# A depthwise convolution computed on even and odd tokens apart, in three half-length filters, without POOL and later in the program

## The chip, the cores and the metric

The program runs on one core of a Trainium2 chip. A core has a matmul engine (PE, with its weight loads shown apart as PEld), three engines for elementwise work (DVE, ACT and POOL) and a queue, SP, that starts most of the transfers from HBM. Each engine works through its own list of instructions in the order in which they stand there, and waits on semaphores for the others. The metric is the time of one execution on the device, in microseconds; lower is better.

## What is computed

One layer of a decoder: 1024 tokens of 1024 channels. A combined input projection feeds four token mixers (a convolution module, latent attention, causal pooling, a gated MLP over chunks); each mixer's output is normalized and goes through its part of `w_out`; a dense squared-ReLU MLP and a last norm follow. The part that the change touches is the convolution module, on 256 of the projected channels (`a`) and 256 gates (`g`):

```python
def conv_module(z, dw_w, dw_b, ln_g, ln_b, pw_w):
    a, g = jnp.split(z, 2, axis=-1)
    y = a * jax.nn.sigmoid(g)
    y = lax.conv_general_dilated(                  # 31 taps, causal, per channel
        y, dw_w[:, None, :], window_strides=(1,), padding=[(CONV_KERNEL - 1, 0)],
        dimension_numbers=('NWC', 'WIO', 'NWC'), feature_group_count=GROUP_WIDTH) + dw_b
    y = jax.nn.silu(layer_norm(y, ln_g, ln_b))
    return y @ pw_w
```

## The kernel before

Everything is float32; a matrix product is made of three matmuls on operands that were split into a high and a low part (`split`: ACT writes the high part, DVE the low one), so each weight that is loaded costs one ACT and one DVE instruction before PE can use it.

The program has two parts. The dense MLP is written in an order made out by hand, from the first product `ffe` on. All that comes before it (projections, mixers, `w_out`) is ordered by a scheduler: the code states what is to be done and in which order of priority, `tc.high_priority(offset=n)` moves a stretch of it ahead by n, and the scheduler lays the instructions of each engine out in one fixed list. Tiles come from rings with few buffers (the tag `K` has 4, `raw` for weights as they come from HBM has 2, `e` and `N` have 1), and a tile takes its turn in its ring.

The names that matter here, in the order in which the work runs:

- `zc`: the products of the convolution's input projection, in four pieces (two groups of 128 channels, `i`, by two halves of the tokens, `hf`). `conv_gate` (L245 to L250) makes the gated input `ycv0`, `ycv1` of them, 128 channels by 1024 tokens each.
- the taps. `tap0` (L313) writes `acc0`, `acc1` = first tap plus bias on ACT, one half of the tokens at a time. A further tap is one DVE instruction, `acc = ycv * weight + acc` on 512 tokens (`conv_taps`, L332, its instruction L337), or, for some taps of group 1, an ACT product into `tap` and an add on POOL (`pool_taps`, L324): 7 taps of the first half and 13 of the second (`NPT`). Of the 120 further taps that leaves 100 for DVE and 20 for POOL. `conv_taps` of the first half stands early in the program with an offset of 2000, that of the second further on with 4000.
- `zp`: the pooling mixer's projection; `zgm` and `zml`: the input projections of the gated MLP and of attention, four products of 48 matmuls each. Their weights `zgm0` to `zgm3`, `zml0` to `zml3` are split as they come. `evac_mla` scales what `zml` gives, `gate` and `ogT` belong to the gated MLP.
- `conv_ln(u)` (L538) for u = 0 to 3, 256 tokens each: PE transposes `acc` (`lnb`), DVE takes mean and variance (`bst`, `bmv`), POOL the root (`lnr`), DVE normalizes (`yn`), PE transposes back (`lnT`), ACT and DVE finish the silu (`vh`, `th`) and split the result into `us`.
- `conv_out` multiplies `us` with the pointwise weights `cw` (`pwc` on PE); `wo` are the products with `w_out`, added to `h` on DVE (L475), `py`, `pw`, `oTp` the pooling mixer's, `cT`, `tl`, `kb`, `qb` attention's preparations.

Of the kernel before, what the change touches and what calls it, by code (L numbers as in the profile page):

```python
# [7 lines left out]
F32 = mybir.dt.float32  # L8
# [9 lines left out]
NRAW = 2  # L18
NB = 8
NM = 2  # L20
NPT = (7, 13)
NWARM = 16
T = 1024
NT = T // P
# [4 lines left out]
GW = 256  # L29
CK = 31  # L30
# [15 lines left out]
C_DWB = 6  # L46
# [11 lines left out]
C_DWW = 61  # L58
# [19 lines left out]
def _trunk(tc, nc, act, dve, pool, pe, sb, ps, hbm, a):  # L78
# [4 lines left out]
    def const(shape, name, dt=F32):  # L83
        return sb.tile(shape, dt, tag=name, name=name)
# [3 lines left out]
    def U(tag, name, shape, dt=F32):  # L88
        return sb.tile([P] + shape, dt, tag=tag, name=name, bufs=BUFS[tag])
# [83 lines left out]
    cols = const([P, NCOL], "cols")  # L173
    ident = const([P, P], "ident")
# [5 lines left out]
    lnhalf = const([P, 4], "lnhalf")  # L180
# [60 lines left out]
    ycv = [None, None]  # L241
    acc = [None, None]

    def conv_gate(i, hf, ba, bg):
        sl = slice(hf * 512, (hf + 1) * 512)  # L245
        th = M("th", [512])
        dve.tensor_mul(th, bg, rb[:, sl])
        dve.scalar_tensor_tensor(ycv[i][:, sl], ba, 0.5, rb[:, sl], ALU.mult, ALU.mult)
        act.activation(th, th, AF.Tanh, scale=0.5)
        dve.scalar_tensor_tensor(ycv[i][:, sl], th, 1.0, ycv[i][:, sl], ALU.add, ALU.mult)  # L250

    wraw, wcm = [], []
    for i in range(2):
# [33 lines left out]
    rb = U("P", "rb", [T])  # L287
# [10 lines left out]
    dve.tensor_scalar(lnhalf, cols[:, C_LNG:C_LNG + 4], 0.5, None, ALU.mult)  # L298

    for i in range(2):  # L300
        ycv[i] = U("P", "ycv%d" % i, [T])
    conv_gate(0, 0, b[:, 0:512], b[:, 512:])
    for i, hf in ((1, 0), (0, 1), (1, 1)):
        if (i, hf) == (0, 1):
            ba, bg = K("zc"), O("zc")
        else:
            b = X("zc")
            ba, bg = b[:, 0:512], b[:, 512:]
# [4 lines left out]
    def tap0(i, hf):  # L313
        if hf == 0:
            acc[i] = U("K", "acc%d" % i, [T])
        sl = slice(hf * 512, (hf + 1) * 512)
        act.activation(acc[i][:, sl], ycv[i][:, sl], AF.Identity,  # L317
                       scale=cols[:, C_DWW + i * CK + CK - 1:C_DWW + i * CK + CK], bias=cols[:, C_DWB + i:C_DWB + i + 1])

    def lag(i, k, hf):  # L320
        lo, hi = max(k, hf * 512), (hf + 1) * 512
        return cols[:, C_DWW + i * CK + CK - 1 - k:C_DWW + i * CK + CK - k], ycv[i][:, lo - k:hi - k], acc[i][:, lo:hi]

    def pool_taps(hf, n):  # L324
        for k in range(1, n + 1):
            c, ya, aa = lag(1, k, hf)
            tap = U("Z", "tap", [512])[:, :ya.shape[1]]
            act.activation(tap, ya, AF.Copy, scale=c)  # L328
            pool.tensor_tensor(aa, aa, tap, ALU.add)  # L329

    def conv_taps(hf, n):
        todo = [(0, k) for k in range(1, CK)]  # L332
        for j, k in enumerate(range(n + 1, CK)):
            todo.insert(2 * j + n + 1, (1, k))
        for i, k in todo:
            c, ya, aa = lag(i, k, hf)
            dve.scalar_tensor_tensor(aa, ya, c, aa, ALU.mult, ALU.add)  # L337

    for hf in range(2):
        tap0(0, hf)  # L340
        tap0(1, hf)
        pool_taps(hf, NPT[hf])

    zp = [None, None]
    for i in range(2):
        w = load_w(a["w_cm"][4 + i], 1024, "wp%d" % i)
        b = X("zp")
# [8 lines left out]
        pool.tensor_scalar(dst[rows, :sh], src[rows, :sh], 1.0, 0.0, ALU.mult, ALU.add)  # L356

    def window_out(win, i):
        rc = small(16, "rc16", 2)
        dve.tensor_mul(rc, win[:, 0:16], cols[:, C_RC + 16 * i:C_RC + 16 * (i + 1)])  # L360
        dve.tensor_sub(rc, rc, zp[i][:, 0:16])
        dve.scalar_tensor_tensor(zp[i], win, cols[:, C_INVW + i:C_INVW + i + 1], zp[i], ALU.mult, ALU.subtract)
        dve.tensor_copy(zp[i][:, 0:16], rc)
# [169 lines left out]

    us = [None, None]

    def conv_ln(u):
        hf = u // 2
        b = K("lnb")  # L538
        for j in range(2):
            for ct in range(2):  # L540
                pe.transpose(b[:, j * GW + ct * P:j * GW + (ct + 1) * P],
                             acc[ct][:, (2 * u + j) * P:(2 * u + j + 1) * P], ident)
        st = small(12, "bst", 2)
        mv = small(4, "bmv", 2)
        for j in range(2):
            dve.bn_stats(st[:, 6 * j:6 * j + 6], b[:, j * GW:(j + 1) * GW])
            dve.bn_aggr(mv[:, 2 * j:2 * j + 2], st[:, 6 * j:6 * j + 6])
        rs = rstd(mv.rearrange("p (j c) -> p j c", c=2)[:, :, 1], 2, "lnr")
        yn = M("yn", [2 * GW])
        for j in range(2):  # L550
            dve.tensor_scalar(yn[:, j * GW:(j + 1) * GW], b[:, j * GW:(j + 1) * GW], mv[:, 2 * j:2 * j + 1],
                              rs[:, j:j + 1], ALU.subtract, ALU.mult)
        b = O("lnT")
        for ct in range(2):
            for j in range(2):
                pe.transpose(b[:, ct * GW + j * P:ct * GW + (j + 1) * P], yn[:, j * GW + ct * P:j * GW + (ct + 1) * P],
                             ident)
        vh = M("vh", [2, GW])
        for ct in range(2):
            act.activation(vh[:, ct, :], b[:, ct * GW:(ct + 1) * GW], AF.Identity, scale=lnhalf[:, ct:ct + 1],  # L560
                           bias=lnhalf[:, 2 + ct:3 + ct])
        th = M("th2", [2, GW])
        act.activation(th, vh, AF.Tanh)
        dve.scalar_tensor_tensor(vh, th, 1.0, vh, ALU.add, ALU.mult)
# [284 lines left out]

    def spare(name):  # L850
        return sb.tile([P, 2, 512], F32, tag="CS", name=name, bufs=1)[:, 0]

    def E(name):
        return sb.tile([P, 512], F32, tag="e", name=name, bufs=1)

    def dram(name, n, dt=F32):
        return hbm.tile([P, n], dt, tag=name, name=name, bufs=1)
# [413 lines left out]
        z_load("zml", 0)  # L1271
    load_h(1)
    with tc.high_priority(offset=2000):
        conv_taps(0, NPT[0])
        z_load("zml", 2)
    with tc.high_priority(offset=1000):
        load_h(2)
# [345 lines left out]
```

## Time and profile before

| | |
|---|---|
| time, median of 3 runs | 1052.73 us (1049.21 to 1052.87) |
| the profiled execution's own time | 1050.52 us |
| its span, from the first to the last instruction | 1048.7 us |
| instructions | 13388 |
| busy: PE, DVE, ACT, POOL | 95%, 81%, 48%, 24% of the span |

The page cuts the span into 40 slices of 26 us; the scheduled part fills the first 15. A group of instructions is given with its count, its busy time, the mean of one, and the idle time of its engine just ahead of it with what ended that. PE's busy time is long by construction: a matmul counts until its result has landed, so neighbours overlap; how fast PE really advances is read from the distance of starts.

### The profile page before, as it was taken

How to read it: one execution, taken by the hardware profiler on the slowest of the kernel's cores; microseconds unless marked ns; L12 is line 12 of the kernel's file. 1: busy time of each engine (PE TensorE's matmuls, PEld its weight loads, DVE VectorE, ACT ScalarE, POOL GpSimd, SP SyncE). 2: the span in 40 equal slices, each digit the busy share in tenths (PEclk: the TensorE clock that was granted, in tenths of full speed). 3: DMA queues.
4: the chain of work that ended last, by engine and by line, in shares of the span. 5: the costliest groups of instructions: out<-in, count | busy, mean ns of one | idle time of the engine just before them, and what ended most of it. 6: DMA issues, size and time to landing. Idle time of an engine off the chain costs nothing.

```text
span 1048.7 us, 13388 instructions
## 1 busy us (share of the span) xinstructions
PE 996.6 (95%) x4674; PEld 819.9 (78%) x4674; DVE 845.9 (81%) x1275; ACT 503.4 (48%) x937; POOL 247.0 (24%) x334
## 2 busy tenths in 40 slices
PE   9994899999999999978999999998999999999996
PEld 7883689888888887756888887886888888888885
DVE  4999999998888666775777775665898988988987
ACT  7641147546568766554445554553251341341334
POOL 0459558323232312211212211221000000000004
PEclk9997899999999999998999999999999999999999
DMA  9411024211002006864666665549949249248004
GB/s 334 155 60 39 30 58 181 78 41 41 1 1 82 1 1 225 302 225 170 232 241 233 228 221 200 202 170 390 392 152 330 81 154 328 81 164 337 1 1 161
DMA packets 49492, 165.71 MB, mean 158 GB/s; under 512 B 6032, under 2 KB 7952, under 8 KB 49424
## 3 DMA queue, kind: packets, MB, share of 16 engines
q1 hardware_dynamic: 36288, 119.68, 32.7%
q0 software_dynamic: 12992, 45.10, 11.1%
q8 instruction: 37, 0.61, 0.2%
q14 instruction: 31, 0.25, 0.1%
q10 hardware_dynamic: 144, 0.07, 0.1%
HBM read 113.45 MB, written 51.38 MB: 157 GB/s over the span
## 4 chain that ended last, share of the span: by engine, by line
PE 65%; DVE 15%; issue 8%; DMA 6%; POOL 3%; ACT 3%; SPq 0%; POOLq 0%; DVEq 0%; ACTq 0%
PE ffb L160 17%; PE ffx L160 13%; PE ffa L160 12%; PE ffy L160 8%; DVE acc L337 8%; PE wo L160 4%; PE ob L160 2%; PE s L676 2%; DMA raw_b<-in_w_ff 1%; PE ptb L719 1%; PE woa L160 1%; DMA xin<-in_x 1%; PE qb L160 1%; DMA wp_raw<-in_w_cm 1%; DVE h L475 1%
## 5 line engine op out<-in xcount | busy, mean ns | idle before, releaser
L160 PE MATMUL ffb<-wop,fop 128*128 128x512 f32 (+1 forms) x780 | 181.4, 392 | 1.0 <-DVE h L1083 1.0
L160 PEld LDWEIGHTS ffb<-wop,fop 128*128 128x128 f32 x780 | 145.2, 188 | 35.5 <-DVE h L1083 1.2
L160 PE MATMUL ffx<-hnT,wop 128*128 128x512 f32 x624 | 151.6, 396 | 5.8 <-ACT ffx L1014 5.0
L160 PEld LDWEIGHTS ffx<-hnT,wop 128*128 128x128 f32 x624 | 118.5, 190 | 33.1 <-ACT ffx L1014 5.5
L160 PE MATMUL ffa<-wop,fop 128*128 128x512 f32 x576 | 137.1, 397 | 3.8 <-DVE h L1083 3.8
L884 DVE TENSOR_TENSOR wop<-w_raw,wop 128x512 fp32r<-128x512 f32 x112 | 76.1, 688 | 72.3 <-ACT wop L881 72.3
L160 PEld LDWEIGHTS ffa<-wop,fop 128*128 128x128 f32 x576 | 109.3, 190 | 29.6 <-DVE h L1083 4.2
L881 ACT ACTIVATE wop<-raw_b 128x512 fp32r<-128x512 f32 x96 | 59.5, 623 | 123.6 <-PE ffa L160 38.4
L337 DVE SCALAR_TENSOR_TENSOR acc<-ycv,cols,acc 128x512 f32<-128x512 f32 (+22 forms) x100 | 99.6, 1038 | 0.6 <-ACT acc L317 0.3
L881 ACT ACTIVATE wop<-w_raw 128x512 fp32r<-128x512 f32 x112 | 68.8, 626 | 43.9 <-DVE w_raw L1027 20.7
L160 PE MATMUL ffe<-hnT,wop 128*128 128x512 f32 x288 | 71.1, 402 | 8.8 <-ACT m L980 8.8
L881 ACT ACTIVATE fop<-raw_f 128x512 fp32r<-128x512 f32 x64 | 39.8, 622 | 75.1 <-DVE h_back L1083 27.6
L884 DVE TENSOR_TENSOR wop<-raw_b,wop 128x512 fp32r<-128x512 f32 x96 | 65.7, 684 | 10.4 <-ACT wop L881 9.7
L1238 POOL TENSOR_SCALAR mr_ms<-mssq,epsr 128x1 f32<-128x1 f32 x7 | 2.8, 399 | 296.9 <-ACT fjunk L1236 296.9
L160 PEld LDWEIGHTS ffe<-hnT,wop 128*128 128x128 f32 x288 | 54.2, 192 | 22.4 <-ACT m L980 10.9
L160 PE MATMUL ffy<-hnB,wop 128*128 128x512 f32 x192 | 46.8, 392 | 0.0
L160 PE MATMUL ffy<-hnT,wop 128*128 128x512 f32 x192 | 46.5, 391 | 0.0
L958 POOL DMA_DIRECT2D fs<-fst x48 | 25.8, 538 | 84.4 <-DVE fst L131 81.0
L884 DVE TENSOR_TENSOR fop<-raw_f,fop 128x512 fp32r<-128x512 f32 x64 | 44.0, 687 | 0.0
L160 PEld LDWEIGHTS ffy<-hnB,wop 128*128 128x128 f32 x192 | 36.0, 188 | 8.2
L160 PEld LDWEIGHTS ffy<-hnT,wop 128*128 128x128 f32 x192 | 36.1, 188 | 7.9
L329 POOL TENSOR_TENSOR acc<-acc,tap 128x512 f32<-128x512 f32 (+7 forms) x20 | 35.2, 1760 | 29.0 <-ACT tap L328 27.7
(450 smaller groups left out, 2153.2 us busy)
## 6 DMA issues: line engine op xcount, KB each, us to landing
fs<-fst POOLq DMA_DIRECT2D x48, 512.0 KB, 3.4
fop<-fs SPq DMA_DIRECT2D x48, 512.0 KB, 6.9
w_raw<-in_w_ff SPq DMA_DIRECT2D x44, 512.0 KB, 4.1
raw_b<-in_w_ff SPq DMA_DIRECT2D x32, 512.0 KB, 5.8
raw_f<-fr SPq DMA_DIRECT2D x32, 512.0 KB, 5.5
fr<-s POOLq DMA_DIRECT2D x32, 256.0 KB, 3.2
fr<-f POOLq DMA_DIRECT2D x20, 256.0 KB, 2.4
xin<-in_x SPq DMA_DIRECT2D x8, 512.0 KB, 8.4
```

The source lines that it names most:

```text
L160: pe.matmul(out, lhs(x), rhs(y), start=start and i == 0, stop=stop and i == 2, skip_group_check=more)
L329: pool.tensor_tensor(aa, aa, tap, ALU.add)
L337: dve.scalar_tensor_tensor(aa, ya, c, aa, ALU.mult, ALU.add)
L475: dve.scalar_tensor_tensor(h[t], b, rs, h[t], ALU.mult, ALU.add)
L676: pe.matmul(sb_[:, c0:c0 + w], q[:, x, qo:qo + P], kt[:, y, 0:w], start=i == 0, stop=i == 2 and not last)
L719: pe.transpose(b[:, place[j] + s * P:place[j] + (s + 1) * P], pts[s][:, (2 * kp + j) * P:(2 * kp + j + 1) * P], ident)
L881: act.activation(self.t[:, 0], self.src(), AF.Copy)
L884: dve.tensor_sub(self.t[:, 1], self.src(), high(self.t))
L958: pool.dma_start(fs[p][q], t.rearrange("p x c -> p (x c)").bitcast(F32))
L1238: pool.tensor_scalar(ms, ssq, 1.0 / D, epsr[:, t:t + 1], ALU.mult, ALU.add)
```

## The change

The 1024 tokens of `ycv` are kept as two rows of 512, even tokens `x0` and odd ones `x1`. With the filter split likewise into even and odd taps, the even outputs are the even taps on `x0` plus the odd taps on `x1` one place back. The odd outputs are not made of two more half-length filters but of one: the even and odd taps are added beforehand (`hsum`, 15 pairs of weights for each group, L331), that filter runs on `x0 + x1`, and the two other results are subtracted. So a group of channels takes three chains of 14 or 15 taps on 512 tokens, in place of four of 15 or 16. The first tap of a chain, where it is a product only, is made on ACT (`acc`, `conv_b`).

No tap goes to POOL any more. `conv_gate` writes `ycv` token pair by token pair, `conv_ln` reads every transposed block from one of the rows, and its `vh` puts even and odd tokens together again. `conv_b` takes the buffer `e`, which had been used by the MLP part alone.

The taps lose both offsets: the whole convolution, with `conv_ln(0)` to `conv_ln(2)` behind it, now stands after the load of `wkv`, far down in the program.

```diff
-NPT = (7, 13)
...
-        dve.scalar_tensor_tensor(ycv[i][:, sl], ba, 0.5, rb[:, sl], ALU.mult, ALU.mult)
+        dve.scalar_tensor_tensor(ba, ba, 0.5, rb[:, sl], ALU.mult, ALU.mult)
         act.activation(th, th, AF.Tanh, scale=0.5)
-        dve.scalar_tensor_tensor(ycv[i][:, sl], th, 1.0, ycv[i][:, sl], ALU.add, ALU.mult)
+        dve.scalar_tensor_tensor(ycv[i].rearrange("p c n -> p n c")[:, hf * 256:(hf + 1) * 256],
+                                 th.rearrange("p (n c) -> p n c", c=2), 1.0,
+                                 ba.rearrange("p (n c) -> p n c", c=2), ALU.add, ALU.mult)
...
-    for hf in range(2):
-        tap0(0, hf)
-        tap0(1, hf)
-        pool_taps(hf, NPT[hf])
...
+    def chain(out, src, taps):
+        for k, c in taps:
+            dve.scalar_tensor_tensor(out[:, k:], src[:, 0:512 - k], c, out[:, k:], ALU.mult, ALU.add)
+
+    def conv_even_odd(i):
+        acc[i] = U("K", "acc%d" % i, [2, 512])
+        x0, x1 = ycv[i][:, 0], ycv[i][:, 1]
+        y0, y1 = acc[i][:, 0], acc[i][:, 1]
+        b = E("conv_b")
+        act.activation(y0, x0, AF.Copy, scale=tap(i, 0))
+        act.activation(b, x1, AF.Copy, scale=tap(i, 1))
+        chain(y0, x0, [(k, tap(i, 2 * k)) for k in range(1, CK // 2 + 1)])
+        chain(b, x1, [(k, tap(i, 2 * k + 1)) for k in range(1, CK // 2)])
+        bias = cols[:, C_DWB + i:C_DWB + i + 1]
+        dve.scalar_tensor_tensor(y1, y0, bias, b, ALU.subtract, ALU.add)
+        dve.tensor_scalar(y0[:, 0:1], y0[:, 0:1], bias, None, ALU.add)
+        dve.scalar_tensor_tensor(y0[:, 1:], y0[:, 1:], bias, b[:, 0:511], ALU.add, ALU.add)
+        dve.tensor_add(x0, x0, x1)
...
+        dve.scalar_tensor_tensor(y1, x0, both(0), y1, ALU.mult, ALU.subtract)
+        chain(y1, x0, [(k, both(k)) for k in range(1, CK // 2)] + [(CK // 2, tap(i, CK - 1))])
...
     with tc.high_priority(offset=2000):
-        conv_taps(0, NPT[0])
         z_load("zml", 2)
...
-    with tc.high_priority(offset=1000):
-        conv_ln(0)
...
     wkv = load_w(a["w_ukv"], 512, "wkv", None, dve)
-    conv_ln(1)
-    with tc.high_priority(offset=4000):
-        conv_taps(1, NPT[1])
-        conv_ln(2)
+    conv_sums()
+    for i in range(2):
+        conv_even_odd(i)
+    for u in range(3):
+        conv_ln(u)
```

Where the scheduler puts the taps is seen in the lists themselves. The first is DVE's, where the chain of the even outputs of group 0 (`acc_1579`, input `ycv_311`) begins. Before, the first taps of group 0 (`acc_481`) stood right behind the gating:

```order
L250 SCALAR_TENSOR_TENSOR ycv_312<-th,ycv_312 128x512
L337 SCALAR_TENSOR_TENSOR acc_481<-ycv_311,cols,acc_481 128x511
L337 SCALAR_TENSOR_TENSOR acc_481<-ycv_311,cols,acc_481 128x510
L337 SCALAR_TENSOR_TENSOR acc_481<-ycv_311,cols,acc_481 128x509
L337 SCALAR_TENSOR_TENSOR acc_481<-ycv_311,cols,acc_481 128x508
L602 TENSOR_TENSOR wsr<-wsr 128x512
```

That was place 30 of DVE's list. Now it is place 102, behind the scaling of `zmla_1357`, which the third of the four `zml` products gives, and behind the low part of `cw`:

```order
L458 TENSOR_SCALAR zmla_1357<-zmla_1357,mr_rs 128x128
L459 TENSOR_SCALAR zmla_1357<-zmla_1357,mr_rs 128x192
L137 SCALAR_TENSOR_TENSOR wo_0l<-wo_0_raw,cols,wo_0h 128x1024
L133 TENSOR_TENSOR cw<-cw_raw,cw 128x512
L335 SCALAR_TENSOR_TENSOR acc_1579<-ycv_311,cols,acc_1579 128x511
L335 SCALAR_TENSOR_TENSOR acc_1579<-ycv_311,cols,acc_1579 128x510
```

Of the 98 convolution instructions on DVE only the 14 of the first `conv_b` chain stand ahead of this place (37 to 57); the other 84 are at places 102 to 207. The second list is ACT's, at the instruction that seeds `acc_1579`, for which the DVE row above waits:

```order
L521 ACTIVATE ogj,ogs<-ug_969 128x256 x2
L132 ACTIVATE oTg_h<-ogT 128x512
L136 ACTIVATE wo_0h<-wo_0_raw,cols 128x1024
L132 ACTIVATE oTg_h<-ogT 128x512
L132 ACTIVATE cw<-cw_raw 128x512
L342 ACTIVATE acc_1579<-ycv_311,cols 128x512
L452 ACTIVATE zmla_1485<-zml,rx 128x352 x2
```

The seed stands at ACT's place 105, behind two transposes of the gated MLP (`ogT`) and behind `cw`; before, `acc_481` and `acc_483` were seeded at ACT's places 33 and 35. The third is PE's list, where it first needs both accumulators finished:

```order
L162 MATMUL wo<-wo_1h,oTp_l 128x512
L604 MATMUL ctb<-ident,zmla_1283 128x128 x2
L604 MATMUL ctb<-ident,zmla_1357 128x128 x2
L557 MATMUL lnb<-ident,acc_1632 128x128
L557 MATMUL lnb<-ident,acc_1579 128x128
L557 MATMUL lnb<-ident,acc_1632 128x128
L572 MATMUL lnT<-ident,yn 128x128 x4
L557 MATMUL lnb<-ident,acc_1579 128x128
```

This is place 848 of PE (`acc_1632` is group 1, whose last tap is at DVE's place 207). The four `conv_ln` blocks, which had stood far apart between `zml` and `wo` products (PE's places 442 to 884), now begin within 40 places of each other (848 to 885), in one stretch with what is left of `ctb`, `pw` and `wo`; the first `pwc` is at 946, where it had been at 961.

More of the change, by code (lines that the diff above doesn't have):

```diff
@@ L111, in N, with E @@
         return sb.tile([P, 512], F32, tag="N", name=name, bufs=1)
+    def E(name):
+        return sb.tile([P, 512], F32, tag="e", name=name, bufs=1)
     def small(n, name, bufs=2):
@@ L300, in _trunk @@
     for i in range(2):
-        ycv[i] = U("P", "ycv%d" % i, [T])
+        ycv[i] = U("P", "ycv%d" % i, [2, 512])
     conv_gate(0, 0, b[:, 0:512], b[:, 512:])
@@ L311, in _trunk @@
         conv_gate(i, hf, ba, bg)
[L313 to L337, printed above, removed]
@@ L339, in _trunk, with tap, conv_sums @@
-    for hf in range(2):
-        tap0(0, hf)
-        tap0(1, hf)
-        pool_taps(hf, NPT[hf])
+    def tap(i, lag_):
+        q = C_DWW + i * CK + CK - 1 - lag_
+        return cols[:, q:q + 1]
+    hsum = const([P, 2 * (CK // 2)], "hsum")
+    def conv_sums():
+        for i in range(2):
+            q = C_DWW + i * CK + 1
+            w = cols[:, q:q + CK - 1].rearrange("p (m c) -> p m c", c=2)
+            dve.tensor_add(hsum[:, i * (CK // 2):(i + 1) * (CK // 2)], w[:, :, 0], w[:, :, 1])
@@ new lines, in chain, with both @@
+    def chain(out, src, taps):
[15 more added lines that the diff above has]
+        dve.tensor_add(x0, x0, x1)
+        def both(k):
+            m = (i + 1) * (CK // 2) - 1 - k
+            return hsum[:, m:m + 1]
+        dve.scalar_tensor_tensor(y1, x0, both(0), y1, ALU.mult, ALU.subtract)
+        chain(y1, x0, [(k, both(k)) for k in range(1, CK // 2)] + [(CK // 2, tap(i, CK - 1))])
@@ L358, in window_out @@
     def window_out(win, i):
-        rc = small(16, "rc16", 2)
+        rc = small(16, "rc16", 1)
         dve.tensor_mul(rc, win[:, 0:16], cols[:, C_RC + 16 * i:C_RC + 16 * (i + 1)])
@@ L541, in conv_ln @@
                 pe.transpose(b[:, j * GW + ct * P:j * GW + (ct + 1) * P],
-                             acc[ct][:, (2 * u + j) * P:(2 * u + j + 1) * P], ident)
-        st = small(12, "bst", 2)
+                             acc[ct][:, j, u * P:(u + 1) * P], ident)
+        st = small(12, "bst", 1)
         mv = small(4, "bmv", 2)
@@ L559, in conv_ln @@
         for ct in range(2):
-            act.activation(vh[:, ct, :], b[:, ct * GW:(ct + 1) * GW], AF.Identity, scale=lnhalf[:, ct:ct + 1],
+            act.activation(vh[:, ct, :].rearrange("p (n c) -> p c n", c=2),
+                           b[:, ct * GW:(ct + 1) * GW].rearrange("p (c n) -> p c n", c=2), AF.Identity, scale=lnhalf[:, ct:ct + 1],
                            bias=lnhalf[:, 2 + ct:3 + ct])
@@ L851, in spare @@
         return sb.tile([P, 2, 512], F32, tag="CS", name=name, bufs=1)[:, 0]
-    def E(name):
-        return sb.tile([P, 512], F32, tag="e", name=name, bufs=1)
     def dram(name, n, dt=F32):
@@ L1309, in _trunk @@
     wkv = load_w(a["w_ukv"], 512, "wkv", None, dve)
-    conv_ln(1)
-    with tc.high_priority(offset=4000):
-        conv_taps(1, NPT[1])
-        conv_ln(2)
+    conv_sums()
+    for i in range(2):
+        conv_even_odd(i)
+    for u in range(3):
+        conv_ln(u)
     with tc.high_priority(offset=300):
```

## The prediction

> **What bounds the kernel now.** I read the slices first, then windows over the scheduled part, then PE's own waits in order of time, then DVE's timeline.
>
> ```profile
> PE   9994899999999999978999999998999999999996
> DVE  4999999998888666775777775665898988988987
> PEclk9997899999999999998999999999999999999999
> ```
>
> ```profile
> 20.00:40.00 20.00, 20.00 (x91) 16.48 (x91) 14.80 (x20) 18.25 (x32) 3.44 (x4) 1.00 0.79 301
> 40.00:60.00 20.00, 20.00 (x91) 16.42 (x90) 19.75 (x21) 6.49 (x11) 10.62 (x8) 1.00 0.17 52
> ...
> 73.40:182.60 109.20, 88.90 (x434) 75.97 (x433) 108.05 (x135) 45.15 (x110) 80.48 (x76) 0.91 0.23 78
> 182.60:234.70 52.10, 51.62 (x262) 43.06 (x262) 47.57 (x71) 28.73 (x51) 17.06 (x23) 1.00 0.19 61
> 234.70:392.00 157.30, 154.94 (x948) 133.64 (x947) 123.69 (x212) 103.68 (x209) 45.56 (x70) 1.00 0.07 21
> ```
>
> The windows give for each stretch its length, then PE, PEld, DVE, ACT and POOL busy, then the granted clock. Over the whole program PE is the bound. From 73.4 to 182.6 it is not: DVE is busy 108.05 of 109.2 us, PE 88.90, at a clock of 0.91. What PE waited for there:
>
> ```profile
> 90.02 0.79 PE L160 MATMUL zgm<-zgm2l,xT_h 128*128 128x512 f32 x1 [9.47 <-DVE zgm2l L131]
> ...
> 103.08 0.50 PE L160 MATMUL zgm<-zgm3l,xT_h 128*128 128x512 f32 x1 [3.45 <-DVE zgm3l L131]
> ...
> 123.20 0.48 PE L541 MATMUL lnb<-ident,acc 128*128 128x128 f32 x1 [4.21 <-DVE acc L337]
> ```
>
> The splits of `zgm2` and `zgm3` came late because DVE had taps ahead of them; the third wait is for taps outright. How much of PE's time this stretch loses follows from its pace:
>
> ```profile
> 73.33 0.40 PE L160 MATMUL zgm<-zgm0h,xT_h 128*128 128x512 f32 x1
> ...
> 164.99 0.33 PE L160 MATMUL zml<-zml0h,xT_h 128*128 128x352 f32 x1
> ...
> 172.92 0.32 PE L160 MATMUL zml<-zml3h,xT_l 128*128 128x352 f32 x1
> ...
> 234.70 0.40 PE L160 MATMUL pwc<-us_h,cw 128*128 128x512 f32 x1
> ...
> 392.04 2.93 PE L160 MATMUL ffe<-hnT,wop 128*128 128x512 f32 x12
> ```
>
> Twelve matmuls on 512 columns in a row last 2.93 us, the last of them 0.39, so (2.93 - 0.39) / 11 = **0.231 us a matmul**. The third `zml` product starts at 164.99 and ends at 173.08 (its last start plus one step of 0.16): 8.1 us for 48 matmuls and four transposes of about 0.11, so 7.65 for the 48. Counting PE's list with these, the work from the first `zgm` (73.33) to the first `pwc` is 131 us, and it took 161.4. About **30 us** are lost to DVE, and that is the most the change can win.
>
> **DVE: what a tap costs.**
>
> ```profile
> L337 DVE SCALAR_TENSOR_TENSOR acc<-ycv,cols,acc 128x512 f32<-128x512 f32 (+22 forms) x100 | 99.6, 1038 | 0.6 <-ACT acc L317 0.3
> ...
> L329 POOL TENSOR_TENSOR acc<-acc,tap x20: 1297/1612/4188, 37.7 to 94.7; 128x512 f32<-128x512 f32 x13, 128x511 f32<-128x511 f32 x1, 128x510 f32<-128x510 f32 x1, 128x509 f32<-128x509 f32 x1
> ...
> 73.67 13.46 DVE L337 SCALAR_TENSOR_TENSOR acc<-ycv,cols,acc 128x492 f32<-128x492 f32 x8
> ...
> 63.36 4.65 DVE L337 SCALAR_TENSOR_TENSOR acc<-ycv,cols,acc 128x495 f32<-128x495 f32 x7
> ...
> 51.60 3.06 DVE L337 SCALAR_TENSOR_TENSOR acc<-ycv,cols,acc 128x501 f32<-128x501 f32 x4
> ...
> 35.30 2.32 DVE L337 SCALAR_TENSOR_TENSOR acc<-ycv,cols,acc 128x511 f32<-128x511 f32 x3 [0.28 <-ACT acc L317]
> ```
>
> Beside POOL's adds eight taps took 13.46 us, 1.68 each; with hardly any POOL work beside them seven took 4.65, (4.65 - 0.74) / 6 = **0.65 each**. Those seven went to accumulators in turn. The three at 35.30 all add to the same one: (2.32 - 0.75) / 2 = **0.785**, so a tap that needs the one just before it costs 0.13 more. (The four at 51.60 give 0.77 between the ones that depend.) A new filter of 98 instructions in place of 100 saves next to nothing by count; taking 20 POOL adds of 1.3 to 1.6 us away gives DVE back some 26 to 32 us.
>
> [...]
>
> **Where the taps go, step by step.** All 84 instructions from place 102 of DVE's list wait for a seed that stands at ACT's place 105, behind the second `ogT` and `cw`. So I work out when that comes.
>
> *PE's third `zml` product ends at about 145.* Up to 73.33 little changes: PE is busy 20 of 20 us in the two windows before it, on `zc` and `zp`, whose splits come no later. Then 192 `zgm` matmuls x 0.231 = 44.4, twenty gate and `ogT` matmuls at about 0.11 = 2.3, three `zml` products = 23.0: 143.0. I add 2 for small waits (the chain of weight loads through one `raw` buffer, the `ang` chain on POOL); from 0 to 6. Before, it ended at 173.08, so PE is 28 us ahead here.
>
> *The seed follows 13 us later.*
>
> ```profile
> 173.28 0.56 ACT L437 ACTIVATE zmla<-zml,rx 128x352 f32<-128x352 f32 x1 [1.09 <-PE zml L160]
> ...
> 178.41 3.61 POOL L148 TENSOR_TENSOR wo_1l<-wo_raw,wo_1h 128x1024 fp32r<-128x1024 f32 x1 [1.06 <-ACT wo_1h L147]
> ...
> 182.05 0.33 SPq L139 DMA_DIRECT2D cw_raw<-in_conv_pw  x1
> ...
> cw_raw<-in_conv_pw SPq DMA_DIRECT2D x1, 256.0 KB, 2.7
> ...
> 191.46 0.62 ACT L130 ACTIVATE cw<-cw_raw 128x512 fp32r<-128x512 f32 x1
> ...
> L317 ACT ACTIVATE acc<-ycv,cols x4: 802/818/820, 34.5 to 63.5; 128x512 f32<-128x512 f32 x4
> ```
>
> `cw_raw` takes its `raw` buffer from a weight that POOL splits (`wo_1l`): before, from the end of the third `zml` (173.08) to its issue 9.0 us, then 2.7 to landing, 0.6 for `cw`, 0.8 for the seed = 13.1. It stands behind eight loads of `h` on SP as before. I take 13; from 8 (the two `ogT` alone) to 15. First tap of the chain: **158**, where it was 35.3. Between 75 and 158 DVE has, counted row by row, 27 us of work: it idles for some 55, and PE runs ahead.
>
> *DVE then needs 76 us to the last tap.* Places 102 to 207 hold 82 wide convolution instructions, 9 additions to `h`, and 15 others.
>
> ```profile
> L475 DVE SCALAR_TENSOR_TENSOR h<-wo,ogr_rs,h 128x1024 f32<-128x1024 f32 x8 | 10.2, 1272 | 0.1
> ...
> L131 DVE TENSOR_TENSOR oTg_l<-ogT,oTg_h 128x512 fp32r<-128x512 f32 x4 | 2.7, 682 | 0.0
> ```
>
> Neighbours overlap by 0.08, so: 82 x 0.655 = 53.7; 9 x 1.2 = 10.8; 15 others (halves of `oTg`, `py`, `ss`, `tl` at 0.6, `wo_1l` 1.2, four scalings of 0.2) = 7.1; sum 71.6. Thirty-seven of the taps follow straight on one that they need, 37 x 0.125 = 4.6. **76.2**, and 1 for waits on `wo`, since only two PSUM tiles carry `wo` and each is freed by an `h` addition in this same list. From 71.6 to 82. Last tap: 158 + 77 = **235**, where it was
>
> ```profile
> 179.67 2.91 DVE L337 SCALAR_TENSOR_TENSOR acc<-ycv,cols,acc 128x512 f32<-128x512 f32 x1
> ...
> 183.77 0.49 PE L541 MATMUL lnb<-ident,acc 128*128 128x128 f32 x3
> ...
> 211.61 0.24 DVE L547 BATCH_NORM_AGGREGATE bmv<-bst 128x2 f32<-128x6 f32 x2
> 211.76 1.25 DVE L475 SCALAR_TENSOR_TENSOR h<-wo,ogr_rs,h 128x1024 f32<-128x1024 f32 x1
> 212.94 0.54 DVE L551 TENSOR_SCALAR yn<-lnb,bmv,lnr_rs 128x256 f32<-128x256 f32 x1
> ```
>
> 182.6. PE stands at its place 848 all this time: with 107 us of work from 73.33 on it would be there by about 181 if nothing held it, and everything behind waits with it.
>
> *From the last tap to the first `pwc`, 30 us.* Places 208 to 248 of DVE add up to 27.2 (eight statistics at 0.33, eight normalizations at 0.45, five `h` at 1.2, the rest halves at 0.6 to 0.7). The first block adds PE's transposes and POOL's root, 1.1 from the end of `bmv` to `yn` (211.85 to 212.94), and a wait for the tanh: 30. From 26 to 38. Before, 52 us lay between the same two points, but PE was full of `wo` work there. First `pwc`: **265**, 30.5 later than 234.70.
>
> *Behind it* the lists hold the same work, 1.3 us more of it on PE, with the windows before at 154.94 busy of 157.3. The MLP part is the same, by hand. Sum: 265 - 234.7 + 1.3 = **+31.6 us**. Against the profiled execution's own time: 1050.52 + 31.6 = 1082.1; the median of the runs, 1052.73, lies 2.2 above it, so I say **1083**.
>
> **Edits that I cost at nothing.** Writing `ycv` by token pairs (4 DVE instructions, 33 to 53 us) and reading pairs in `vh` (8 on ACT): the trace shows no element-wise stride; from nothing to twice the time, 2.8 us on DVE, covered by its idle time, and 4 us on ACT in the tail, which is within that term's range. `hsum` and the one-column addition, 0.2 each. Single buffers for `rc16` and `bst`: reader and writer are both DVE, in order. Twenty `tap` products less on ACT: it is 28.73 of 52.10 busy, no bound.
>
> **Rivals.**
>
> 1. *Faster: DVE's relief reaches PE.* 26 to 32 us of DVE come free and the `zgm` splits come in time; if the last tap were done when PE gets to place 848, near 181, all 30 us of loss would go: 1021. For it speak the three PE waits. Against it: the seed's place, which holds back 84 taps until 158. It decides if that seed came by 104 (181 - 77). SBUF — State Buffer, section "Who interferes with whom", in the Trainium skill backs its premise, a DVE instruction with two inputs in SBUF and a POOL one that reads SBUF block each other whole; the 1.68 against 0.65 agrees.
> 2. *No change:* a seed by 126, with the loss only moved: 1050. It needs `cw` and both `ogT` ahead of PE's own pace, which 143 forbids. Nothing speaks for it.
> 3. *Slower, but taken back in part:* between 234.7 and 392.0 PE's work at its pace is 136 us of 157.3; if those 20 us are DVE backlog that shifts away, up to 15 come back: 1068. DVE's 123.69 of 157.3 speaks against a backlog.
> 4. *Slower still, by the clock:* PE starves from 160 to 265, and when it starved before, the clock fell (slice 4 at 0.7; `zgm2h` below took 493 ns against 394). If PE runs the tail's 23 us of work so, 6 to 15 more: 1090 to 1098.
>
> ```profile
> L160 PE MATMUL zgm<-zgm2h,xT_h 128*128 128x512 f32 x16 | 7.9, 493 | 0.7 <-ACT zgm2h L130 0.7
> L160 PE MATMUL zgm<-zgm0h,xT_h 128*128 128x512 f32 x16 | 6.3, 394 | 0.0
> ```
>
> **How the numbers follow.** Forecast 0.63, rival 3 0.15, rival 4 0.14, rival 1 0.04, rival 2 0.04. All the low ends of the terms at once (143, 8, 71.6, 26) give 1066 and all the high ones (149, 15, 82, 38) 1101; with the two slower rivals the range is 1063 to 1100. A measurement of this kernel tells 0.5%, 5 us, from no change: faster 0.04, same 0.04, slower 0.92.
>
> **What would show it.** ACT's first write of `acc` near 157; the last L335 near 235; L335 at a mean of 0.75 us or less, where L337 had 1.04; no PE wait for `zgm2l` or `zgm3l`; PE's idle time ahead of `lnb` and of the `wo` matmuls between 160 and 260; first `pwc` near 265, first `ffe` near 424. It is wrong if the seed comes before 130 or the last tap before 210.

## The result, and the profile after

The changed kernel takes **1099.69 us** (median of 4 runs, 1096.03 to 1100.10); the kernel before, run beside it, 1050.97 (4 runs, 1048.69 to 1052.87). The ratio is **1.0457**, with a 95% interval of 1.0422 to 1.0492: slower. The forecast was 1083 in a range of 1063 to 1100; the direction and the main mechanism were right, and the median lies 0.3 us inside the upper end of the range. The profiled execution took 1096.03 us, the shortest of the four, with a span of 1094.2 (before: 1050.52 and 1048.7). So the parts below have to add up to +45.5, where the forecast had +31.6.

The slices of the profile page of the changed kernel, in the order in which the prediction read them:

```profile
PE   9999983618999999997899999999899999999996
DVE  5674359888688876588677776656798988988987
PEclk9999997758899999999899999999999999999999
```

A slice is 27 us. PE is full in slices 0 to 4, where slices 3 and 4 held it up before. Then come 8, 3, 6, 1 and 8 tenths in slices 5 to 9 (137 to 274 us), where it had been full, and the granted clock in slices 6 to 9 is 0.7, 0.7, 0.5 and 0.8. DVE now idles ahead of this: it is busy 4, 3 and 5 tenths of slices 3 to 5.

The same in windows of the changed kernel (length, then busy time of PE, PEld, DVE, ACT and POOL, then the granted clock, the share of the DMA engines and GB/s):

```profile
73.40:155.00 81.60, 80.46 (x426) 71.37 (x425) 34.43 (x52) 36.90 (x98) 42.83 (x61) 1.00 0.28 96
...
180.00:200.00 20.00, 0.06 (x1) 0.00 (x0) 19.93 (x32) 0.29 (x1) 0.00 (x0) 0.50 0.00 0
200.00:220.00 20.00, 18.08 (x78) 14.46 (x78) 15.52 (x21) 4.52 (x7) 1.49 (x1) 0.91 0.00 1
220.00:240.00 20.00, 0.69 (x2) 0.29 (x2) 19.20 (x28) 0.00 (x0) 0.00 (x0) 0.51 0.00 0
240.00:260.00 20.00, 11.91 (x50) 9.19 (x51) 14.45 (x32) 12.00 (x19) 3.46 (x7) 0.63 0.02 3
...
280.00:300.00 20.00, 18.58 (x72) 15.05 (x73) 11.46 (x20) 8.26 (x19) 3.32 (x4) 0.74 0.00 0
```

From 73.4 to 155 PE hardly waits: 80.46 busy of 81.60, with 1.1 us of waits for `zml3`. DVE works 34 us of 82. In two later windows (180 to 200, 220 to 240) PE stands almost completely still while DVE is full. Its waits from 150 to 260, grouped by what it waited for (total, times, longest):

```profile
PE wo L162 <- DVE oTg_l L133: 20.0, 1, 20.0
PE lnb L557 <- DVE acc L335: 11.7, 1, 11.7
PE lnb L557 <- DVE acc L349: 11.6, 2, 10.3
PE wo L162 <- DVE h L490: 7.3, 4, 3.2
PE lnT L572 <- ACT us_h L132: 3.7, 1, 3.7
PE lnT L572 <- DVE yn L567: 2.7, 1, 2.7
```

The two waits for `acc` are the ones that the prediction named. It looked for idle time ahead of `wo` too, but the longest wait was not in its working: 20.0 us for `oTg_l`, the low part of the transposed gated-MLP output. The timelines of ACT and DVE show where that comes from:

```profile
154.55 0.63 ACT L132 ACTIVATE cw<-cw_raw 128x512 fp32r<-128x512 f32 x1 [2.29 <-DMA cw_raw<-in_conv_pw]
155.09 0.71 ACT L342 ACTIVATE acc<-ycv,cols 128x512 f32<-128x512 f32 x1
...
203.05 0.69 ACT L136 ACTIVATE oTp_h<-pw,cols 128x512 fp32r<-128x512 f32 x1 [22.76 <-PE pw L162]
...
207.53 0.72 ACT L342 ACTIVATE acc<-ycv,cols 128x512 f32<-128x512 f32 x1 [0.55 <-DVE py_l L133]
```

```profile
155.83 5.89 DVE L335 SCALAR_TENSOR_TENSOR acc<-ycv,cols,acc 128x511 f32<-128x511 f32 x5
...
198.57 0.73 DVE L335 SCALAR_TENSOR_TENSOR acc<-ycv,cols,acc 128x497 f32<-128x497 f32 x1
199.34 1.29 DVE L133 TENSOR_TENSOR oTg_l<-ogT,oTg_h 128x512 fp32r<-128x512 f32 x2
203.77 0.75 DVE L137 SCALAR_TENSOR_TENSOR oTp_l<-pw,cols,oTp_h 128x512 fp32r<-128x512 f32 x1 [3.14 <-ACT oTp_h L136]
205.61 1.28 DVE L490 SCALAR_TENSOR_TENSOR h<-wo,ogr_rs,h 128x1024 f32<-128x1024 f32 x1 [1.09 <-PE wo L162]
...
229.22 10.88 DVE L335 SCALAR_TENSOR_TENSOR acc<-ycv,hsum,acc 128x511 f32<-128x511 f32 x14
240.13 0.73 DVE L335 SCALAR_TENSOR_TENSOR acc<-ycv,cols,acc 128x497 f32<-128x497 f32 x1
```

The seed comes right behind `cw`, as forecast, at 155.09. From 180 to 199 DVE runs through taps; only then does it reach `oTg_l`, for which PE has stood since 180. PE's next rows (`wo`, then `pw`) come too late for ACT's `oTp_h`, and DVE, which has `oTp_l` next, now waits 3.14 us for ACT, which had waited for PE. It is a loop: DVE's list holds up PE, and PE's lateness holds up DVE's list. The seed of the second group comes only at 207.53, behind `py_l`, which reads `zp`; `zp` is in a buffer of tag `K` too, and the second accumulator seems to take it over.

Where the marks of the prediction lie in the two profiles (first tap: the first of the chain of even outputs, y0; last tap: its end; the forecast of 143.5 is 142.23 + 1.3):

| | before | forecast | after |
|---|---|---|---|
| first tap | 35.3 | 158 | 155.83 |
| last tap, end | 182.6 | 235 | 240.86 |
| first `pwc` | 234.70 | 265 | 275.22 |
| from there to the first `ffe` | 142.23 | 143.5 | 149.94 |
| span | 1048.7 | +31.6 | 1094.2 (+45.5) |

### The profile page after: what moved, and what is told of

Its sections match the earlier page's. It is cut to its first block, busy times and chain, and to the rows that moved or that the text cites. A ratio compares the mean times of both kernels' runs of the same rounds, so it can differ in the third digit from the quotient of the medians.

```text
span 1094.2 us, 13333 instructions
## 1 busy us (share of the span) xinstructions
PE 1002.6 (92%) x4674; PEld 823.6 (75%) x4674; DVE 820.1 (75%) x1275; ACT 491.0 (45%) x917; POOL 196.8 (18%) x314
## 4 chain that ended last, share of the span: by engine, by line
PE 78%; DVE 8%; issue 6%; DMA 3%; ACT 3%; POOL 2%; SPq 0%; POOLq 0%; DVEq 0%; ACTq 0%
PE ffb L162 16%; PE ffx L162 13%; PE ffa L162 12%; PE ffy L162 7%; PE wo L162 6%; PE zgm L162 4%; PE zc L162 4%; DVE acc L335 3%; PE s L693 2%; PE ob L162 2%; PE zml L162 2%; PE zp L162 2%; PE ptb L736 1%; DMA raw_b<-in_w_ff 1%; DVE h L490 1%
## 5 line engine op out<-in xcount | busy, mean ns | idle before, releaser
L693 PE MATMUL s<-kb,qT 128*128 128x512 f32 (+2 forms) x144 | 33.2, 362 | 0.7 <-DVE h L490 0.7
L1138 DVE TENSOR_TENSOR raw_f<-raw_f,raw_f 128x512 f32<-128x512 f32 x48 | 32.8, 685 | 0.6 <-DMA raw_f<-fr 0.6
```

The source lines that it names most:

```text
L693: pe.matmul(sb_[:, c0:c0 + w], q[:, x, qo:qo + P], kt[:, y, 0:w], start=i == 0, stop=i == 2 and not last)
L1138: dve.tensor_sub(self.r[d, i], self.r[x, i], self.r[y, i])
```

## The experiments

The theory on record has three parts: the place of the seeds behind `cw` costs the time; from the seed on the DVE list sets the end; the new filters, at the old place, would win up to the 30 us that PE lost to DVE. Against it stood: the chains that depend on themselves cost the time; the low priority costs it; the clock costs it. Each ratio is against the kernel before on the same chip, so to be compared with 1.0457.

**1 and 2. Place and filters apart.** First the old filters, POOL taps included, at the new place:

```diff
-            tap = U("Z", "tap", [512])[:, :ya.shape[1]]
+            tap = sb.tile([P, 512], F32, tag="e", name="tap", bufs=1)[:, :ya.shape[1]]
...
-    for hf in range(2): tap0(0, hf); tap0(1, hf); pool_taps(hf, NPT[hf])
...
     wkv = load_w(a["w_ukv"], 512, "wkv", None, dve)
+    for hf in range(2):
+        tap0(0, hf); tap0(1, hf); pool_taps(hf, NPT[hf]); conv_taps(hf, NPT[hf])
+    for u in range(3): conv_ln(u)
```

> The filters and the POOL taps of before, stated where the change states its convolution and with no priority of their own; the buffer of a POOL tap comes from another tag. Theory A (the place costs the time: the seeds stand behind the cw load): first seed near 157, the taps behind it, 1080 to 1110 us. Theory B (the new filters cost it: their chains depend on themselves): with the old filters the time returns to 1045 to 1055.

1127.73 us, ratio 1.0708 (1.0690 to 1.0726). The first tap starts at 158.3, the last at 293.1. Theory A holds, and the loss is above its band: with two accumulators to be finished by 100 taps and 20 POOL adds the late place costs 28 us more than with the new filters. Part of this may be the run's own: its products for POOL have one buffer where they had four before, so ACT and POOL took turns (216.9 to 267.0). DVE waited for POOL only 3.2 us there; how much of the 28 us it is was not tried.

Then the new filters at the old place:

```diff
+        acc[i] = U("K", "acc%d" % i, [2, 512])   # ahead of zp
...
     with tc.high_priority(offset=2000):
+        conv_sums()
+        for i in range(2): conv_even_odd(i)
         z_load("zml", 2)
...
+    with tc.high_priority(offset=1000): conv_ln(0)
...
+    conv_ln(1)
+    with tc.high_priority(offset=4000): conv_ln(2)
```

> The new filters, stated where before stated its taps, at the priority of before (2000), with the first conv_ln blocks at their old places. Theory A (the place): the seeds come near 40 to 70, no PE wait for zgm2l or zgm3l, last tap before 190, and up to the 30 us that PE lost to DVE before are won: 1018 to 1035 us. Theory B (the new filters): no better than 1050, since 98 instructions that depend on each other replace 100 that don't.

1052.75 us, ratio 1.0004 (0.9992 to 1.0016): no difference from before. (Here as in all runs the kernel before took 1050.7 to 1052.3 us beside it.) The whole loss is the place's, by which two things are meant that this run moves together: the priority, and the turn of the accumulators for their buffers, which they now take ahead of `zp` and `cw`. But theory A's other half fell: nothing was won either. Theory B has the number, but not the reason, that dependent taps cost as much as those that they replace: the 88 taps of L335 take DVE 70.6 us in all, where the 100 before took 99.6. Four numbers, then:

| | place of before | new place |
|---|---|---|
| filters of before | 1052.30 | 1127.73 |
| new filters | 1052.75 | 1099.69 |

**3. What holds the seeds: the priority, or the ring of buffers?** One statement of the changed kernel is moved, and loses its own priority. `cw` and the accumulators share the four buffers of tag `K`, which are handed out in order.

```diff
-    with tc.high_priority(offset=1000):
-        cw = small_w(load_raw(a["conv_pw"], 512, "cw_raw"), 512, "K", "cw")
...
     for i in range(2): conv_even_odd(i)
+    cw = small_w(load_raw(a["conv_pw"], 512, "cw_raw"), 512, "K", "cw")
```

> The changed kernel, its low priority kept, with one statement moved: the cw load stands behind conv_even_odd and without priority, so that the accumulators come ahead of cw in the ring of K buffers. Theory A1 (what holds the seeds is the ring, not the priority): the seeds go to ACT's places near 42, the DVE list becomes nearly that of the new filters at the early place, and the time is within 8 us of that run: 1018 to 1040. Theory A2 (the low priority holds them): no change, 1090 to 1102 us.

1049.30 us, ratio 0.9973 (0.9959 to 0.9987). ACT's timeline of this kernel:

```profile
75.12 1.07 ACT L132 ACTIVATE zgm3h<-zgm_raw 128x1024 fp32r<-128x1024 f32 x1 [9.98 <-PE zp L162]
76.09 1.32 ACT L342 ACTIVATE acc<-ycv,cols 128x512 f32<-128x512 f32 x2
```

Both seeds now start at 76, the first of them 79 us earlier, at the same low priority: A2 falls, and the load of `cw` ahead of them is what held them. That it did so by its turn in the ring, as A1 has it, agrees with two more rows of the changed kernel: the seed of `conv_b`, stated beside them at the same low priority but in a buffer of another tag, ran at 48.2, and the second seed waited for the reader of `zp`. A run in which `cw` only takes another buffer was not made. The 50 us of this change hang on where one load stands. (A1's band of 1018 to 1040 was missed, by the same relief that doesn't pay in run 2; within 8 us of that run it is.)

**4 to 6. Why doesn't DVE's relief pay at the early place?** POOL's part alone, in the kernel before:

```diff
-NPT = (7, 13)
+NPT = (0, 0)
```

> The kernel before with all 120 taps on DVE and none on POOL. Theory A (POOL's adds slow DVE's taps from 0.65 to 1.68 us): DVE has 20 x 0.65 = 13 us more to do and gets 26 to 32 back, so 13 to 19 less in all: 1032 to 1042 us, taps at a mean of 0.75 or less. Rival (DVE is simply the bound there and gets 13 us more): 1058 to 1066.

1049.21 us, ratio 0.9969 (0.9956 to 0.9983). That is some 3 us faster, and both bands were missed: the mean tap is 0.86 us in place of 1.04, but 120 of them keep DVE as busy as before (105.29 us of the window below). Next, every second tap of a chain is left out on top of run 2 (42 of 88, not the 44 of the expectation; the kernel then leaves out part of the convolution), and then run 2 gets earlier seeds:

```diff
-        for k, c in taps:
+        for k, c in taps[::2]:
```

> The new filters at the early place with every second instruction of each chain left out (44 of 88 remain; the convolution is not computed in full). Theory D (before 182 us DVE is what PE waits for, and relief would be worth the 30 us that the prediction put on it, if there were enough of it): 44 x 0.8 = 35 us less on DVE, the last tap before 150, the time 1018 to 1030. Rival (something else, the loads or PE's own list, takes the place of the taps): 1040 or more.

```diff
         acc[i] = U("K", "acc%d" % i, [2, 512])
+        act.activation(acc[i][:, 0], ycv[i][:, 0], AF.Copy, scale=tap(i, 0))
...
-        act.activation(y0, x0, AF.Copy, scale=tap(i, 0))
```

> The new filters at the early place, and the first product of each y0 chain stated right behind its gate, so that it no longer stands behind zgm3h on ACT: first y0 taps near 50 in place of 76, into time in which DVE was idle (49 to 76, some 10 us). Theory D (relief on DVE reaches PE): 5 to 10 us less than the new filters at the early place, 1042 to 1048 us. Rival: the taps now stand ahead of the zgm splits as before, and the wait for zgm2l is back: 1050 to 1058.

Half the taps: 1036.48 us, ratio 0.9857 (0.9838 to 0.9876). Earlier seeds (first at 50.5): 1050.81, ratio 0.9989 (0.9976 to 1.0003), no difference. The same window of three kernels, the kernel before, run 2 and the one with half the taps:

```profile
73.40:180.00 106.60, 86.30 (x417) 73.37 (x416) 105.44 (x134) 43.63 (x107) 77.97 (x75) 0.90 0.24 80
```

```profile
73.40:180.00 106.60, 92.85 (x460) 80.87 (x458) 100.41 (x143) 44.07 (x109) 66.32 (x68) 0.94 0.24 81
```

```profile
73.40:180.00 106.60, 96.51 (x480) 83.55 (x480) 85.35 (x121) 48.93 (x123) 57.77 (x72) 0.95 0.24 80
```

With the new filters DVE is still busy 100.41 of 106.6 us: its relief here is 5 us, not 26 to 32. The rest is taken up by taps that the kernel before runs ahead of the window, from 35 on: the new chains need a whole group of `ycv` (there at 48), and in run 2 the seeds of y0 stand behind `zgm3h` on ACT and come at 74.5, so DVE is busy only 18.6 of the 24.4 us from 49 to 73.4, where before it was busy 37.8 of the 38.4 from 35 on. POOL, without its taps, is still busy for 66.32 us, and beside it thirteen taps at 81.6 took 14.0 us, 1.08 each. And PE's gain is handed back: 92.85 against 86.30 by 180, yet the first `pwc` stands at 234.09 where it was at 234.70. The waits of PE in run 2, from 73 to 235:

```profile
PE gate L506 <- ACT gv_h L132: 6.8, 1, 6.8
PE wo L162 <- DVE h L491: 5.8, 2, 2.9
PE zml L162 <- DVE zml3l L133: 2.9, 1, 2.9
```

The 9.47 us for `zgm2l` are gone; waits for `gv_h`, `h` and `zml3l` came in their place. With half the taps the gain does come, about 14 to 16 us for 29 us of taps taken out (the taps of L335 take 70.6 us in run 2, 41.6 here). Neither its band nor the rival's was met: it is less than one for one. Earlier seeds alone brought other waits (6.9 us for `acc` ahead of `lnb`); the time is in the rival's band, but the wait for `zgm2l` that it expected is not there. Which list order would pass the relief on to PE in full stays open.

**7. Does the DVE list set the end one for one at the late place?** The same halving as in run 5, now in the changed kernel, where most of the taps left out lie behind the seed.

> The changed kernel with every second instruction of each chain left out (the convolution is not computed in full). Of the 42 left out, 35 lay behind the seed at 155.8. Theory A (at the late place the DVE stretch sets the end one for one): 35 x 0.70 = 24.5 us less, and some of the waits in it: last tap at 210 to 217, first pwc at 245 to 253, 1067 to 1076 us. Rival (PE's own list, or the tail, takes the place of the taps, as with the half filters at the early place, where 35 us less on DVE gave 16): 1080 or more.

1074.98 us, ratio 1.0225 (1.0198 to 1.0251): 24.7 below the changed kernel's 1099.69. DVE's and PE's timelines:

```profile
218.54 0.74 DVE L335 SCALAR_TENSOR_TENSOR acc<-ycv,cols,acc 128x497 f32<-128x497 f32 x1
```

```profile
253.28 0.40 PE L162 MATMUL pwc<-us_h,cw 128*128 128x512 f32 x1
```

This execution is 3 us later than the other ahead of this stretch (its first `zgm` starts at 76.32, not 73.23), which is also why the last tap and the first `pwc` are just outside theory A's bands. Counted from the first `zgm` the last tap is 24.7 us earlier, the first `pwc` 25.0, the end 23.9, for 35 taps of 0.70: one for one. Theory A is shown. The same filters with half their taps save 25 us at one place and 14 to 16 at the other.

**8. Is the excess of the DVE stretch its waits?** The remainder of the second `oTg` is taken from DVE:

```diff
-            split(oT[0][:, ct, :], oT[1][:, ct, :], b)
+            if hf == 1:
+                oc = N("oc")
+                act.activation(oT[0][:, ct, :], b, AF.Copy)
+                act.activation(oc, b, AF.Copy)
+                pool.tensor_sub(oT[1][:, ct, :], oc, oT[0][:, ct, :].bitcast(F32))
```

> The changed kernel with the remainder of the second oTg (two halves) taken from DVE: ACT copies the transposed block to SBUF and POOL subtracts, so that the wo matmuls after the first lnb no longer wait for place 160 of DVE. The order lists then also free the second accumulator's buffer sooner, so that the two chains alternate more. Theory A (the 8 us that the DVE stretch took beyond the forecast are its waits for PE, which itself waits for oTg_l): PE's wait of 20 us after the first lnb goes, the last tap comes at 230 to 236 in place of 240, the time falls by 4 to 10 us: 1087 to 1093 us. Rival (DVE's list is full whatever PE does): last tap within 2 us of 240, time within 3 us of 1097.

1091.51 us, ratio 1.0389 (1.0363 to 1.0414). The last tap starts at 233.29: theory A's numbers. But PE's wait did not go, it is 24.8 us now and for POOL's `oTg_l`, which ran at 212.2 and 214.6. What the edit did was the other thing in the expectation: the second seed came at 166.75, not 207.53, so the chains alternate and DVE has other work at hand. DVE's stretch from first to last tap in the changed kernel, and in this one:

```profile
155.83:240.86 85.03, 33.44 (x131) 24.94 (x131) 77.87 (x108) 10.95 (x21) 7.66 (x10) 0.72 0.06 17
```

```profile
157.00:234.02 77.02, 34.34 (x128) 25.85 (x128) 75.76 (x105) 10.67 (x22) 10.58 (x12) 0.76 0.07 20
```

Busy time 77.87 against 75.76, idle time 7.2 against 1.3. Most of the 8 us is idle time of DVE inside its own list, and it is gone where DVE hardly waits for ACT and PE. The rest isn't a clean comparison: this list has two `oTg_l` (1.3 us) less, and its alternating taps of L335 take 51.7 us in place of 54.5. PE's wait for `oTg_l` doesn't add to the end by itself: here it is longer, and the kernel is faster. In the changed kernel its price, as far as is seen, is what it made DVE wait.

**9 and 10. Is it the clock?** Matmuls whose results nobody reads are put into PE's list behind the first and second `lnb`; the other lists stay as they are.

```diff
                 pe.transpose(b[:, j * GW + ct * P:j * GW + (ct + 1) * P], acc[ct][:, j, u * P:(u + 1) * P], ident)
+                if u == 0 and j == 0:
+                    fill((44, 22)[ct], acc[ct][:, 0, 0:GW])
```

This is the edit of run 10, where `fill(n, src)` issues `n` matmuls on `src` into a part of the `lnb` bank that is written later; run 9 issues 22 and 14 at the same places.

> The changed kernel with 36 matmuls whose results nobody reads (22 behind the first lnb, 14 behind the second, 256 columns of f32) in PE's list, all other lists as they are. They fill PE's waits of 20 and 12 us. Theory C (PE's low clock after its long waits costs 6 to 15 us in the tail and behind the first pwc): the granted clock from 200 to 300 goes to 0.9 or more, from last tap to first pwc 30 us or less, the time falls by 5 to 12: 1085 to 1092 us. Rival (the tail waits for round trips through DVE, POOL and ACT, not for PE's pace): clock higher, time within 3 us of 1097.

> The changed kernel with 66 idle matmuls (44 behind the first lnb, 22 behind the second, 256 columns of f32, 0.43 us each in the run before), so that the waits of 20 and 12 us are full to within 2 us. Theory C (the low clock in the tail comes from these two waits): the granted clock from 240 to 260 rises from 0.63 to 0.85 or more, and the time falls by 4 to 9 us to 1088 to 1094. Rival C2 (the clock of the tail is set by the short waits in the tail itself): 240 to 260 stays at 0.7 or less, the time within 4 us of the changed kernel.

22 and 14: 1100.30, ratio 1.0466 (1.0446 to 1.0486), no gain. 44 and 22: 1094.93, ratio 1.0416 (1.0392 to 1.0440), whose interval just meets the changed kernel's. Windows of the latter:

```profile
180.00:200.00 20.00, 18.69 (x80) 15.95 (x79) 19.96 (x33) 0.72 (x1) 0.00 (x0) 0.91 0.00 1
220.00:240.00 20.00, 10.68 (x42) 9.15 (x43) 19.23 (x27) 0.00 (x0) 0.00 (x0) 0.74 0.00 1
240.00:260.00 20.00, 11.43 (x48) 8.74 (x47) 14.23 (x32) 11.21 (x18) 2.66 (x6) 0.74 0.00 0
280.00:300.00 20.00, 18.54 (x94) 15.00 (x94) 15.73 (x27) 12.04 (x23) 4.19 (x4) 1.00 0.00 1
```

The clock from 240 to 260 rose only from 0.63 to 0.74, and from last tap to first `pwc` it took 35.7 us against 34.4: in the tail PE waits for DVE, POOL and ACT in turn, and what clock was gained there bought nothing. The clock of 0.74 meets neither C's condition (0.85 or more) nor C2's (0.7 or less), so the tail at full clock wasn't seen. From 280 to 300 the clock is 1.00 in place of 0.74, and from first `pwc` to first `ffe` it takes 145.8 us against 149.9. So the low clock costs that stretch about 4 us; that it comes from the idle stretches ahead is likely by this run. For the whole program the gain isn't shown: the timed intervals meet, and in the profiled execution the stretch from the first `ffe` to the end is 3.1 us longer than in the changed kernel, with 8.2 us of waits for ACT's `m` in place of 5.6, so that its span, 1095.3, is no shorter than 1094.2.

**11 and 12. A version that beats both.** In runs 3 and 4 DVE was still behind most of what PE waited for (in run 3 the longest wait, 7.3 us, was for ACT's `gv_h`, which had waited for DVE's `vg`), so 16 small scalings go to ACT in each:

```diff
-        dve.tensor_scalar(z[:, 0:128], z[:, 0:128], rs[:, 0:1], None, ALU.mult)
-        dve.tensor_scalar(z[:, 128:320], z[:, 128:320], rs[:, 1:2], None, ALU.mult)
+        act.activation(z[:, 0:128], z[:, 0:128], AF.Copy, scale=rs[:, 0:1])
+        act.activation(z[:, 128:320], z[:, 128:320], AF.Copy, scale=rs[:, 1:2])
```

> The kernel with cw behind the seeds, and the 16 scalings of zmla (0.2 to 0.3 us each on DVE) on ACT. Theory D (DVE still sets PE's waits before 180): 4 us less on DVE, of which half reaches PE as with the half filters: 1046 to 1048 us, faster than both kernels. Rival (ACT's copies for gv_h and zml3h come later): 1049 to 1053.

> The kernel before with all taps on DVE, and the same 16 scalings on ACT. Theory D: 2 to 3 us less than without that, 1046 to 1048 us. Rival: 1049 to 1053.

1045.21 us, ratio **0.9936** (0.9916 to 0.9955), with the new filters, and 1046.64, ratio 0.9951 (0.9931 to 0.9971), with the old ones: about as theory D had it (the first 0.8 us below its band), and both faster than the two kernels of this study, by 0.5 to 0.6% of the kernel before. In the first the wait for `gv_h` stayed (7.1 us), and those for `h` fell from 3.6 to 0.9. In the second the step itself isn't shown: its interval meets that of run 4. The intervals of the two meet as well; that the new filters are better than the old ones isn't shown even here.

## Why the prediction was right, and where its sizes were off

The path was right: the seed behind `cw`, then DVE's list, then the first `pwc`, and what follows. The place inside the range is in part luck. In three places the kernel took 18.8 us longer than forecast, in two 4.9 less, which keeps it just inside; and the stretch of DVE, 85.0, lies above the 82 at which its own range ended.

- **PE's pace up to the third `zml`: right.** It was to end at 145 with 2 us of small waits, and ends at 144.5; the window from 73.4 to 155 has 80.46 busy of 81.60, and the waits for `zgm2l` and `zgm3l` are gone.
- **The seed 13 us later, first tap at 158: right**, 155.83, 2.2 early. That the seed stands behind `cw` is the cause: run 3 moves `cw` alone and the loss is gone. (DVE's work from 73.4 to 155 is 34.4 us, where 27 were counted from 75 to 158; DVE was idle enough for it to cost nothing.)
- **DVE 77 us to the last tap: the mechanism right (run 7, one for one), the size wrong by 8.0.** The term that was too small is "1 for waits on `wo`". The stretch took 85.0, of which 77.87 busy, 1.7 over the forecast of 76.2, and 7.2 idle. The busy excess is mainly the five first taps, (5.89 - 0.75) / 4 = 1.29 each, while POOL works on `zmla` and the low part of `wq`. Of the idle time 5.5 us stand as waits in DVE's own view of waits:

```profile
DVE oTp_l L137 <- ACT oTp_h L136: 3.1, 1, 3.1
DVE h L490 <- PE wo L162: 2.4, 3, 1.1
```

  The prediction counted `wo`'s two tiles, but let PE stand "at its place 848 all this time". PE stood 20 us at an earlier place, for an `oTg_l` behind the taps, and DVE then waited for what PE hadn't done. Run 8 without that loop: 77.0 us. That this is the forecast's own number is chance, since its list has less to do (see there).
- **The tap that needs the one before it: right.** (10.88 - 0.75) / 13 = 0.779 in the changed kernel. In run 8, where two chains alternate, this row gives (3.37 - 0.75) / 4 = 0.655:

```profile
172.14 3.37 DVE L335 SCALAR_TENSOR_TENSOR acc<-ycv,cols,acc 128x504 f32<-128x504 f32 x5
```

- **30 us from the last tap to the first `pwc`: short by 4.4**, within its 26 to 38. The forecast added 2.8 us of waits to DVE's own 27.2; PE's waits for `yn` and `us_h` alone, round trips through DVE, POOL and ACT, are 2.7 and 3.7. Raising the clock there from 0.63 to 0.74 (run 10) didn't shorten it; what a full clock would do was not seen.
- **"Behind it the lists hold the same work", 1.3 us: wrong by 6.4.** The 1.3 us more of work on PE is there: the first `pwc` now stands ahead of six `vb` matmuls on 256 columns (0.12 us) and three `kb` on 512 (0.23) that it stood behind before, 1.4 us. The other 6.4 us had no term in the forecast. Of them 1.8 are waits of PE, mainly for `qT` and `vt_l` (3.5 us in the stretch, 1.7 before). About 4 are the clock from 280 to 300, the mechanism of rival 4 with a smaller price than its 6 to 15, and at another place than the tail. From the first `ffe` on the kernel gains 2.7 us, with shorter waits for `m` (5.6 us in place of 8.8). (The prediction's mark of 392.04 for `ffe` is a run of twelve, not the first; that run begins at 440.24, where it said 424.)
- **The sum:** 31.6 - 2.2 + 8.0 + 4.4 + 6.4 - 2.7 = 45.5. (Two slips in the prediction's arithmetic change little: 265 is 30.3 behind 234.70, not 30.5, and its sum used 30.3; and 1082.1 with the 2.2 that it names is 1084.3, not 1083.)
- **Rival 1: its condition was right to be denied, its price was wrong.** It was to decide if the seed came by 104, and to give 1021. In run 2 the seeds come at 74.5 and the last tap starts at 178.8, ahead of PE's 181, and the time is 1052.75. The sentence on "the most the change can win" took all of PE's lost time for a prize; run 2 shows that the waits move on. DVE's relief was taken for 26 to 32 us out of the rows beside POOL's taps, but the window had 5.
- **Rivals 2 and 3** were rightly put low: between `pwc` and `ffe` nothing was taken back, that stretch got longer; only 2.7 us came back behind it.

## What to carry to other kernels

Before a priority is blamed for a late instruction, look at who is ahead of it in the ring that hands out its buffer: here one load of a weight, stated earlier and not needed until much later, held back 84 instructions of DVE, and one moved line undid the loss. A term "waits" in a sum for one engine's list has to follow the loop: what the other engine waits for in this list is what this list will wait for next. And an idle stretch of the bounding engine is worth what it can give back only if the work behind it is ready; take some work out altogether (half the taps) to see what relief is worth before counting on it.

## What the runs showed of the hardware

- Writing `ycv` in token pairs, alternately to two rows of the tile, took 1.10 us a half (L253, median of four) where the plain write took 0.69 (L250 before): 1.6 times. (L253 also reads an operand from `zc` that L250 didn't; L251 in the same kernel does so too, with a plain write, and takes 0.69.) The prediction had put it between one and two times.
- PE has two paces here. From 288.42 to 291.41 `wo` matmuls on 512 columns follow each other at 0.43 us, and from 292.23 on at 0.23, with nothing else changed:

```profile
288.42 0.63 PE L162 MATMUL wo<-wo_0h,oTp_h 128*128 128x512 f32 x1
288.85 0.63 PE L162 MATMUL wo<-wo_0l,oTp_h 128*128 128x512 f32 x1
...
292.23 0.39 PE L162 MATMUL wo<-wo_1h,oTp_h 128*128 128x512 f32 x1
292.47 0.40 PE L162 MATMUL wo<-wo_1l,oTp_h 128*128 128x512 f32 x1
```

  TensorE: Matmul & The Clock Gate, section "What's actually happening", in the Trainium skill has the gate at half or full rate by how busy PE has been recently. The steps of 0.43 and 0.23 agree, near enough, with half and full. In run 10 the granted clock was 0.91 in the window of the first fill of 20 us and 1.00 in the next, and 0.74 in the window behind the second fill of 11 us, in which PE waits 2.7 and 3.7 us. No run here measures how long "recently" is.
